# Weight sums of a second projection, formed by transfers in device memory ahead of their use

## The chip, the cores and the metric

The kernel runs on one core of a Trainium2 chip. The metric is the device time of one execution in microseconds (us). A core has the engines TensorE (PE in the profile, with its weight loads as PEld), VectorE (DVE), ScalarE (ACT), GpSimd (POOL) and SyncE (SP), each with its own queue, worked off in order, and 16 transfer engines (DMA) that serve the transfers which SP, ACT and POOL issue. Here SP issues plain transfers and POOL those that add to what stands at their target. SBUF is the memory on the core, PSUM the memory that TensorE writes its products to; inputs and outputs lie in device memory.

## The reference

One layer of a streaming encoder on 1024 tokens of width 1024, in float32:

```python
hn = rmsnorm(h, norm_mix_g[i])
z = hn @ w_in[i]                               # 1024 x 2048
a = pool_mixer(u, pool_w[i], pool_b[i], pool_scale[i])
o = chunk_attention(q, k, v, rel_bias[i])      # 8 heads, own chunk of 64 and 8 before
h = h + jnp.concatenate([a, o], axis=-1) @ w_out[i]
hn = rmsnorm(h, norm_ffn_g[i])
up = hn @ w_up[i]                              # 1024 x 5632: gate, value
gt, val = up[..., :D_FF], up[..., D_FF:]
gt = causal_dwconv(gt, conv_w[i], conv_b[i])
h = h + (jax.nn.gelu(gt, approximate=False) * val) @ w_down[i]   # 2816 x 1024
hn = rmsnorm(h, norm_ple_g[i])
gate = jax.nn.sigmoid(hn @ w_ple_gate[i] + b_ple_gate[i])
h = h + gate * (p[i] @ w_ple[i])
return rmsnorm(h, final_g)
```

The change concerns the product with `w_down`, called the second projection here; the product with `w_up` is the first.

## The kernel before

Everything is kept transposed: channels on the 128 partitions, tokens along the rows. Each float32 factor is split into a rounded part on ACT and a remainder on DVE (`split`, L132 to L134), and a product of two such factors takes three matmuls of 128x128 by 128x512 (`mm3`, L128 to L130).

*Stages.* After the loads and the first norm comes the attention stage (to about 260 us). A loop over 64 pairs of head and token tile puts scores, exponentials and values in order; pieces of the input projection fill TensorE between them. Each head's bias rows are loaded by `load_bias` (SP L319), negated by ACT (L320), and two corners are set by POOL (L321, L322), one head ahead, into one of two buffers; a buffer is free when the head before last is done with it. `load` (SP L180) brings each block of `w_in` and `w_v` into one of two buffers. POOL raises the first norm's sums to the power -0.5 (L246), and clears a few columns ahead of the pooling groups (L443), which are written much later, in `project_u`.

*First projection.* 22 column blocks (`up(fi)`, each with a gate and a value half) are multiplied by the scheme of Strassen and Winograd: the operand of tokens and the weights are cut in quarters, and seven products (`step(fi, n)`, 84 matmuls a block) take the place of eight. POOL adds the quarters of `w_up` in SBUF (L710). Each block's result, GELU of the gate times the value, goes to device memory as one tile of `GD` (SP L869).

*Second projection.* The same scheme on `w_down`, with depth 2816 cut into two halves of 11 tiles. Seven products of 11 steps, 12 matmuls a step, in the order 1, 5, 6, 3, 7, 2, 4, add into PSUM. With w(i,j) the four quarters of the weights, products 5, 6, 3 and 7 need sums:

- product 5: w(2,1) + w(2,2); product 6: that + w(1,1); product 3: that + w(1,2);
- product 7: w(2,1) + w(1,1).

Product 1, 2 and 4 use w(1,1), w(1,2) and w(2,2) themselves. For 5, 6 and 3, `SW(k)` is a resident SBUF tile: loaded in product 5, grown by an adding transfer from POOL (`grown`, L893), and after each use grown again for the next product (`behind`). Product 7 loads a tile and lets one transfer add to it. The other operands are tiles of `GD`: T(k), B12(k) and B22(k) stay in SBUF and are formed into differences by DVE (`later_sums`, L943 to L947), B21 is loaded in product 2. In product 1 the B12 tiles 0 to 6 are loaded all at once, at step 6, and one a step behind that. `ready` issues loads 6 steps ahead, `formed` splits 2 ahead and does the sums of a step 4 steps later (`LAG`). The loads of the gate's weights and their splits (`gate_weights`) are hung into products 7 and 2, and the regions of SBUF that they go to are named anew by `weights_home` and `behind_7`.

*What sets the order.* Only TensorE's order is that of the code (`tc.manual_schedule`). For the other engines a planner runs through the program once and puts on each queue, whenever that queue is free by its reckoning, the instruction that is ready and stands earliest in the code; what is not ready is passed by. A transfer counts there by its size alone, whether it loads, stores, copies or adds. On the chip the order so found is fixed: an instruction that has to wait holds up its queue. `load_to` calls `tc.keep_in_program_order` on its loads once `pinned` is set, behind the first projection, which ties each to the instruction traced before it on SP. Names of the profile: R, B and F are SBUF regions, PS is PSUM, TB and V hold parts of the tokens' operand.

Of the kernel before, what the change touches and what calls it, by code (L numbers as in the profile page):

```python
# [20 lines left out]
NF = FF // P  # L21
# [62 lines left out]
def trunk(tc, xT, pT, vecs, w_qk0, w_in, w_v, bias, counts, pool_w, w_out, w_up, w_down,  # L84
# [4 lines left out]
    with tc.tile_pool(name="sb", bufs=1) as sb, \  # L89
# [14 lines left out]
        small = sb.tile([P, 80], F32, name="small")  # L104
        PS = pp.tile([P, 8, 512], F32, name="PS")
        GD = dr.tile([NF, P, SEQ], F32, name="GD")

        b_pool = tc.tile_pool(name="b1", bufs=1)
        B = b_pool.__enter__().tile([P, 8192], F32R, name="B")
# [653 lines left out]
        for z, d in enumerate((0, 4, 1, 5, 2, 6, 3, 7)):  # L763
            k = z // 2
# [33 lines left out]
        def step(fi, n):  # L798

            x, y, z, w = firsts.get(fi, (0, 1, 2, 3))  # L800
            product({1: x, 2: x, 5: z, 3: z, 6: y, 7: y, 4: w}[n], n not in (2, 3, 7))
            if n == 1 and fi != 1:
                keep(np1, x, -1.0)
            elif n == 2 and fi:
                gate0(x)
                if fi in halved:
                    gate(fi, HS[0])
            elif n == 5:
                keep(rawd if fi == 1 else V[:, HS[1]], z)
# [48 lines left out]
        def up(fi, hook=None):  # L858
            if fi == 0:
                pool.memset(Gb[:, 0:2], 0.0)  # L860
                gate0(firsts[0][0])
            if fi == 1:
                keep(np1, firsts[1][0], -1.0)
            for n in steps[fi]:
                step(fi, n)
                if hook and n == 6:
                    hook()
            values_in(slice(0, SEQ))
            sp.dma_start(GD[fi], Yb)  # L869

# [4 lines left out]
        def raw_buf(which="w"):  # L875
            turn[which] += 1
            return rings[which][turn[which] % len(rings[which])]

        def load_to(dst, src):
            ins = sp.dma_start(dst, src)  # L880
            if pinned[0]:
                tc.keep_in_program_order(ins)
            return dst

        def gated(k, i, j):

            return GD[k + NK * (i - 1), :, HS[2 - j]]

        def weight(k, i, j):
            return w_down[k + NK * (j - 1), :, (i - 1) * 512:i * 512]  # L890

        def grown(dst, k, i, j):
            pool.dma_start(dst, weight(k, i, j), accum_op=ALU.add)  # L893
            return dst

        def T(k):
            return r(2 * k, 512)

        def SW(k):
            return r(96 + 2 * k, 512)  # L900

        def B12(k):
            return r(32 + 2 * k, 512)

        def B22(k):
            return r(64 + 2 * k, 512)

        def operands(n, k):

            if n == 1:  # L910
                if pinned[0]:
                    for z in range(0 if k == READY else k, k + 1):
                        load_to(B12(z), gated(z, 1, 2))
                return load_to(raw_buf(), weight(k, 1, 1)), load_to(T(k), gated(k, 1, 1))
            if n == 5:
                grown(load_to(SW(k), weight(k, 2, 1)), k, 2, 2)
                load_to(B22(k), gated(k, 2, 2))
                return SW(k), T(k)
            if n == 6:
                return SW(k), T(k)  # L920
            if n == 3:
                return SW(k), B22(k)
            if n == 7:
                return grown(load_to(raw_buf(), weight(k, 2, 1)), k, 1, 1), B12(k)
            if n == 2:
                b21[k] = load_to(raw_buf("g"), gated(k, 2, 1))
                return load_to(raw_buf(), weight(k, 1, 2)), b21[k]
            return load_to(raw_buf(), weight(k, 2, 2)), T(k)

        def behind(n, k):  # L930

            if n == 5:
                grown(SW(k), k, 1, 1)
            elif n == 6:
                grown(SW(k), k, 1, 2)
            elif n == 2:
                dve.tensor_tensor(T(k), T(k), b21.pop(k), ALU.subtract)

        def later_sums(n, k):

            tt = dve.tensor_tensor
            if n == 1:
                tt(T(k), T(k), B12(k), ALU.add)  # L943
            elif n == 5:
                tt(T(k), T(k), B22(k), ALU.subtract)
            elif n == 6:
                tt(B12(k), B12(k), B22(k), ALU.subtract)  # L947
# [5 lines left out]
        pinned, b21 = [False], {}  # L953
        ORDER = (1, 5, 6, 3, 7, 2, 4)
        sequence = [(n, k) for n in ORDER for k in range(NK)]
        READY, FORMED, LAG = 6, 2, 4
        got, made = {}, [0, 0]

        def ready(upto):
# [4 lines left out]
        def formed(upto):  # L964
            while made[1] < min(upto, len(sequence)):
                i = made[1]
                w_, g_ = got.pop(i)
                (split_neg if sequence[i][0] in (5, 6) else split)(g_, *g_form[i % 3])
                split(w_, *w_form[i % 4])
                behind(*sequence[i])  # L970
                if i >= LAG:
                    later_sums(*sequence[i - LAG])
                made[1] += 1

        def first_steps():
# [4 lines left out]
        for fi in range(NF):  # L980
            up(fi, first_steps if fi == NF - 1 else None)
        pinned[0] = True
        for z in (1, 2, 3, 4):
            Rs[z] = region(z, F32)
        rings["g"] = [r(b, 512) for b in range(22, 32, 2)]

# [66 lines left out]
        emptied = []  # L1053
# [155 lines left out]
```

## Time and profile before

| | us |
|---|---|
| runs shown (three) | 1169.34, 1169.53, 1166.51; median 1169.34 |
| profiled execution, its own time | 1163.96 |
| its span, first to last instruction | 1162.2 |
| TensorE busy | 1133.5 |
| DVE, ACT, POOL busy | 896.2, 581.6, 249.7 |
| second projection on TensorE | about 801 to 1032 |

The profile is one execution. In a row by stretches stand: the stretch in us from the span's start, its length, the busy time and count of PE, PEld, DVE, ACT and POOL, the granted share of TensorE's clock, the mean busy share of the 16 transfer engines, and GB/s. A row of waits has engine and line, what it waited for, us in total, times, longest. A row in order of time has start, duration, engine, line, operation, target and source, count, and in brackets the idle time before it and what ended it. "SPq" is SP issuing a transfer; "issue" is time in which an engine waited for nothing that the profile shows. A row of transfer issues has count, size and the median time from issue to landing.

### The profile page before, as it was taken

How to read it: one execution, taken by the hardware profiler on the slowest of the kernel's cores; microseconds unless marked ns; L12 is line 12 of the kernel's file. 1: busy time of each engine (PE TensorE's matmuls, PEld its weight loads, DVE VectorE, ACT ScalarE, POOL GpSimd, SP SyncE). 2: the span in 40 equal slices, each digit the busy share in tenths (PEclk: the TensorE clock that was granted, in tenths of full speed). 3: DMA queues.
4: the chain of work that ended last, by engine and by line, in shares of the span. 5: the costliest groups of instructions: out<-in, count | busy, mean ns of one | idle time of the engine just before them, and what ended most of it. 6: DMA issues, size and time to landing. Idle time of an engine off the chain costs nothing.

```text
span 1162.2 us, 15566 instructions
## 1 busy us (share of the span) xinstructions
PE 1133.5 (98%) x5697; PEld 957.3 (82%) x5697; DVE 896.2 (77%) x1396; ACT 581.6 (50%) x1019; POOL 249.7 (21%) x224
## 2 busy tenths in 40 slices
PE   9999999999999999999999999999879999999996
PEld 7988998888888778888888888888757887888996
DVE  7678877879557679999989999988747578974553
ACT  8568687755555434344343433444324465663342
POOL 0000000082013213333434343431135010000000
PEclk9999999999999999999999999999889999999998
DMA  7110101105410361212121222224999265510011
GB/s 261 38 48 30 49 12 67 39 28 181 146 28 10 74 162 61 103 64 100 64 101 64 100 73 91 87 76 140 363 228 151 42 186 179 190 54 1 29 65 53
DMA packets 55660, 111.45 MB, mean 96 GB/s; under 512 B 6304, under 2 KB 8608, under 8 KB 55584
## 3 DMA queue, kind: packets, MB, share of 16 engines
q1 hardware_dynamic: 47376, 95.71, 23.4%
q0 software_dynamic: 8064, 14.68, 7.6%
q8 instruction: 44, 0.72, 0.2%
q14 instruction: 32, 0.26, 0.1%
q10 hardware_dynamic: 144, 0.07, 0.0%
HBM read 94.71 MB, written 15.73 MB: 95 GB/s over the span
## 4 chain that ended last, share of the span: by engine, by line
PE 78%; DMA 7%; DVE 5%; issue 5%; ACT 2%; POOL 1%; SPq 0%; DVEq 0%; POOLq 0%; ACTq 0%
PE PS L129 23%; PE PS L128 23%; PE PS L130 23%; PE PS L366 2%; DVE R L134 2%; DMA R<-in_w_down 2%; PE PS L383 1%; PE PS L384 1%; DMA F<-in_w_up 1%; DMA R<-GD 1%; DMA F<-in_w_down 1%; DMA F<-in_w_gate 1%; POOL R L893 1%; DVE B L134 1%; PE PS L341 1%
## 5 line engine op out<-in xcount | busy, mean ns | idle before, releaser
L128 PE MATMUL PS<-R,R 128*128 128x512 f32 (+1 forms) x944 | 361.9, 383 | 1.6 <-ACT V L796 1.5
L130 PE MATMUL PS<-R,R 128*128 128x512 f32 (+1 forms) x944 | 358.0, 379 | 0.0
L129 PE MATMUL PS<-R,R 128*128 128x512 f32 (+1 forms) x880 | 340.1, 387 | 0.3 <-DVE R L229 0.3
L134 DVE TENSOR_TENSOR R<-F,R 128x512 fp32r<-128x512 f32 (+1 forms) x214 | 189.6, 893 | 26.6 <-ACT R L133 25.9
L130 PEld LDWEIGHTS PS<-R,R 128*128 128x128 f32 x944 | 177.6, 188 | 34.0 <-DVE R L134 0.4
L128 PEld LDWEIGHTS PS<-R,R 128*128 128x128 f32 x944 | 177.7, 188 | 33.8 <-ACT V L796 2.0
L133 ACT ACTIVATE R<-F 128x512 fp32r<-128x512 f32 (+1 forms) x218 | 132.3, 621 | 142.8 <-PE PS L129 81.5
L129 PEld LDWEIGHTS PS<-R,R 128*128 128x128 f32 x880 | 165.7, 188 | 32.2 <-DVE R L229 1.1
L710 POOL TENSOR_TENSOR F<-F 128x512 f32<-128x512 f32 x76 | 142.9, 1880 | 221.9 <-DVE R L134 138.7
L128 PE MATMUL PS<-B 128*128 128x512 f32 x316 | 126.1, 399 | 10.6 <-ACT B L133 5.6
L129 PE MATMUL PS<-B 128*128 128x512 f32 x316 | 126.3, 400 | 2.4 <-DVE B L134 1.2
L130 PE MATMUL PS<-B 128*128 128x512 f32 x316 | 125.3, 397 | 0.0
L134 DVE TENSOR_TENSOR B<-R,B 128x512 fp32r<-128x512 f32 x88 | 59.4, 686 | 36.5 <-ACT B L133 36.2
L133 ACT ACTIVATE B<-R 128x512 fp32r<-128x512 f32 x88 | 53.8, 623 | 61.0 <-PE PS L129 31.6
L128 PEld LDWEIGHTS PS<-B 128*128 128x128 f32 x316 | 60.7, 192 | 25.7 <-ACT B L133 6.9
L129 PEld LDWEIGHTS PS<-B 128*128 128x128 f32 x316 | 60.6, 192 | 19.0 <-DVE B L951 3.3
L129 PE MATMUL PS<-B,R 128*128 128x256 f32 x256 | 72.2, 282 | 0.0
L130 PEld LDWEIGHTS PS<-B 128*128 128x128 f32 x316 | 60.5, 191 | 12.9 <-DVE B L134 0.6
L352 ACT ACTIVATE F<-F,small 128x640 f32<-128x640 f32 (+2 forms) x64 | 44.4, 694 | 21.0 <-DVE small L350 12.8
L128 PE MATMUL PS<-B,R 128*128 128x256 f32 x192 | 54.5, 284 | 0.0
L130 PE MATMUL PS<-B,R 128*128 128x256 f32 x192 | 54.4, 283 | 0.0
L608 ACT ACTIVATE F<-F 128x512 f32<-128x512 f32 (+1 forms) x49 | 27.8, 568 | 47.8 <-DVE F L1112 24.3
(164 smaller groups left out, 1920.1 us busy)
## 6 DMA issues: line engine op xcount, KB each, us to landing
F<-in_w_up SPq DMA_DIRECT2D x91, 256.0 KB, 2.7
GD<-F SPq DMA_DIRECT2D x22, 512.0 KB, 2.6
F<-in_w_down SPq DMA_DIRECT2D x44, 256.0 KB, 4.6
R<-GD SPq DMA_DIRECT2D x44, 256.0 KB, 5.4
R<-in_w_down POOLq DMA_DIRECT2D x33, 256.0 KB, 5.2
F<-in_w_in SPq DMA_DIRECT2D x10, 512.0 KB, 3.5
F<-in_xT SPq DMA_DIRECT2D x16, 256.0 KB, 6.0
F<-in_w_out SPq DMA_DIRECT2D x16, 256.0 KB, 2.8
```

The costliest lines, as they stand in the source:

```text
L128: pe.matmul(ps, ahi, bhi, start=first, stop=False, skip_group_check=more)
L129: pe.matmul(ps, ahi, blo, start=False, stop=False, skip_group_check=more)
L130: pe.matmul(ps, alo, bhi, start=False, stop=last, skip_group_check=more)
L133: act.activation(hi, src, AF.Copy)
L134: dve.tensor_tensor(lo, src, rv(hi), ALU.subtract)
L341: pe.matmul(PS[:, 4 + z, 0:320], q, K1[:, ks], start=False, stop=True)
L352: act.activation(S[:, 0:n], S[:, 0:n], AF.Exp, bias=s_[:, 0:1], scale=-1.0, accum_out=s_[:, 1:2])
L366: pe.transpose(pst[:, j * P:(j + 1) * P], S[:, j * P:(j + 1) * P], ident)
L383: pe.matmul(O, V[:, k, h], pt[:, 0, idx], start=n_ == 0, stop=False)
L384: pe.matmul(O, V[:, k, h], pt[:, 1, idx], start=False, stop=n_ == len(ks) - 1)
L608: act.activation(self.q, src, AF.Square)
L710: pool.tensor_tensor(rawu[to], rawu[a], rawu[b], op)
```

## The change

Four stacks of 11 tiles in device memory, `SD`, hold the sums, and the second projection loads them like plain weights. `weight_sums(k, part)` makes those of one k in six parts, and in the code the parts stand behind the steps of the first projection, part by part in later column blocks (blocks 2 to 17). Its copies are issued by SP, its adding transfers by POOL; none of them is passed to `tc.keep_in_program_order`.

```diff
+        SD = [dr.tile([NF // 2, P, 512], F32, name=f"SD{n}") for n in range(4)]
...
-            for n in steps[fi]:
+            for z, n in enumerate(steps[fi]):
                 step(fi, n)
+                for part in range(6):
+                    k = fi - 2 - part
+                    if z == part and 0 <= k < NK:
+                        weight_sums(k, part)
...
-        def grown(dst, k, i, j):
-            pool.dma_start(dst, weight(k, i, j), accum_op=ALU.add)
-            return dst
+        def weight_sums(k, part):
+
+            s1, s2, s4, s3 = [t[k] for t in SD]
+
+            def grow(t, i, j):
+                pool.dma_start(t, weight(k, i, j), accum_op=ALU.add)
+            if part == 0:
+                sp.dma_start(s1, weight(k, 2, 1))
+                sp.dma_start(s3, weight(k, 2, 1))
+            elif part == 1:
+                grow(s1, 2, 2)
+                grow(s3, 1, 1)
+            elif part == 2:
+                sp.dma_start(s2, s1)
+            elif part == 3:
+                grow(s2, 1, 1)
+            elif part == 4:
+                sp.dma_start(s4, s2)
+            else:
+                grow(s4, 1, 2)
+
+        def weight_sum(n, k):
+            return SD[{5: 0, 6: 1, 3: 2, 7: 3}[n]][k]
...
+            z = {1: k - READY, 5: k + NK - READY}.get(n, -1)
+            if 0 <= z < NK:
+                load_to(B12(z), gated(z, 1, 2))
             if n == 1:
-                if pinned[0]:
-                    for z in range(0 if k == READY else k, k + 1):
-                        load_to(B12(z), gated(z, 1, 2))
                 return load_to(raw_buf(), weight(k, 1, 1)), load_to(T(k), gated(k, 1, 1))
-            if n == 5:
-                grown(load_to(SW(k), weight(k, 2, 1)), k, 2, 2)
-                load_to(B22(k), gated(k, 2, 2))
-                return SW(k), T(k)
...
-                return grown(load_to(raw_buf(), weight(k, 2, 1)), k, 1, 1), B12(k)
+            if n in (5, 6, 3, 7):
+                if n == 5:
+                    load_to(B22(k), gated(k, 2, 2))
+                return load_to(raw_buf(), weight_sum(n, k)), {5: T, 6: T, 3: B22, 7: B12}[n](k)
...
-            if n == 5:
-                grown(SW(k), k, 1, 1)
-            elif n == 6:
-                grown(SW(k), k, 1, 2)
-            elif n == 2:
+            if n == 2:
...
-        READY, FORMED, LAG = 6, 2, 4
+        READY, FORMED, LAG, LAG_1 = 6, 2, 4, 8
...
-                if i >= LAG:
+                if i >= LAG and sequence[i - LAG][0] != 1:
                     later_sums(*sequence[i - LAG])
+                if i >= LAG_1 and sequence[i - LAG_1][0] == 1:
+                    later_sums(*sequence[i - LAG_1])
...
-        for z in (1, 2, 3, 4):
+        for z in (1, 2, 3):
...
         def behind_7():
-            weights_home(2, 32, range(4, 8))
-            Rs[3] = region(3, F32R)
-            hp[0] = [(r(64 + 4 * k, 512), r(66 + 4 * k, 512)) for k in range(KT)]
+            Rs[2] = region(2, F32R)
+            hp[0] = [(r(32 + 4 * k, 512), r(34 + 4 * k, 512)) for k in range(KT)]
...
-        extra = {(3, 10): lambda: weights_home(4, 96, range(4)), (7, 10): behind_7,
-                 (4, 8): norm_a.sums, (4, 9): lambda: norm_a.rows(rst2[:, HS[0]])}
-        for k, at in enumerate([(7, b) for b in (1, 3, 5, 7)] + [(2, b) for b in (1, 3, 5, 7)]):
+        extra = {(6, 10): lambda: weights_home(4, 96, range(4)), (3, 10): lambda: weights_home(3, 64, range(4, 8)),
+                 (7, 10): behind_7, (4, 8): norm_a.sums, (4, 9): lambda: norm_a.rows(rst2[:, HS[0]])}
+        for k, at in enumerate([(3, b) for b in (1, 3, 5, 7)] + [(7, b) for b in (1, 3, 5, 7)]):
```

`SW` goes. B12's tiles are loaded one a step over eleven steps, the sums of product 1's operands are made 8 steps behind instead of 4, and the gate's weights move from products 7 and 2 to products 3 and 7, into regions that are free earlier because `SW` is gone.

More of the change, by code (lines that the diff above doesn't have):

```diff
@@ L890, in weight @@
             return w_down[k + NK * (j - 1), :, (i - 1) * 512:i * 512]
-        def grown(dst, k, i, j):
-            pool.dma_start(dst, weight(k, i, j), accum_op=ALU.add)
-            return dst
+        def weight_sums(k, part):
[18 more added lines that the diff above has]
+            return SD[{5: 0, 6: 1, 3: 2, 7: 3}[n]][k]
         def T(k):
             return r(2 * k, 512)
-        def SW(k):
-            return r(96 + 2 * k, 512)
         def B12(k):
@@ L908, in operands @@
         def operands(n, k):
+            z = {1: k - READY, 5: k + NK - READY}.get(n, -1)
+            if 0 <= z < NK:
+                load_to(B12(z), gated(z, 1, 2))
             if n == 1:
-                if pinned[0]:
-                    for z in range(0 if k == READY else k, k + 1):
-                        load_to(B12(z), gated(z, 1, 2))
                 return load_to(raw_buf(), weight(k, 1, 1)), load_to(T(k), gated(k, 1, 1))
-            if n == 5:
-                grown(load_to(SW(k), weight(k, 2, 1)), k, 2, 2)
-                load_to(B22(k), gated(k, 2, 2))
-                return SW(k), T(k)
[L919 to L923, printed above, removed]
-                return grown(load_to(raw_buf(), weight(k, 2, 1)), k, 1, 1), B12(k)
+            if n in (5, 6, 3, 7):
+                if n == 5:
+                    load_to(B22(k), gated(k, 2, 2))
+                return load_to(raw_buf(), weight_sum(n, k)), {5: T, 6: T, 3: B22, 7: B12}[n](k)
             if n == 2:
```

## The prediction

> **What bounds the kernel now.** I read the page's busy times first, then the stretches around the second projection, then what the engines there wait for, and last the queues of SP, ACT and POOL in the first 80 us, because the transfers that the change adds depend on nothing written late.
>
> ```profile
> PE 1133.5 (98%) x5697; PEld 957.3 (82%) x5697; DVE 896.2 (77%) x1396; ACT 581.6 (50%) x1019; POOL 249.7 (21%) x224
> 720.00:800.00 80.00, 80.00 (x354) 66.27 (x353) 72.34 (x79) 32.81 (x48) 30.32 (x16) 1.00 0.29 102
> 800.00:840.00 40.00, 36.80 (x148) 29.12 (x147) 29.98 (x44) 14.80 (x23) 4.39 (x5) 0.91 0.79 261
> 840.00:880.00 40.00, 32.07 (x119) 23.36 (x119) 24.63 (x41) 12.56 (x22) 16.56 (x19) 0.91 1.00 222
> 880.00:920.00 40.00, 40.00 (x177) 32.83 (x176) 25.66 (x42) 17.03 (x30) 13.05 (x15) 1.00 0.68 109
> 960.00:1000.00 40.00, 38.20 (x166) 30.60 (x165) 36.25 (x60) 26.25 (x48) 0.00 (x0) 1.00 0.60 208
> ```
>
> TensorE is the bound nearly everywhere: 354 matmuls fit into 80 us before the second projection and 177 into 40 us after its worst part, 0.226 us each. Only 800 to 880 falls out: 148 + 119 = 267 matmuls where 354 would fit. The 87 missing ones are 19.7 us. The idle time alone would be 11.1 us; the rest is the granted clock, 0.91. At 960 to 1000, 11 are missing, 2.5 us. So what the second projection can give back is about 22 us.
>
> ```profile
> ACT B L133 <- DMA R<-in_w_down: 27.6, 11, 6.0
> ACT B L133 <- DMA F<-in_w_down: 14.3, 6, 9.6
> 853.82 0.86 POOL L893 DMA_DIRECT2D R<-in_w_down  x1 [3.63 <-issue]
> ```
>
> ACT's splits wait there for weights, above all for those that POOL adds into SBUF (R<-in_w_down), while the transfer engines are fully busy (share 1.00). That is the place the change works on.
>
> **The change part by part.** *The second projection.* The 44 adding transfers leave it. Products 1 and 2 now read 33 + 22 = 55 plain tiles of 256 KB (product 1: weight, T, and B12, whose last six slide into product 2; product 2: s1 and B22). That is 14.4 MB in about 60 us, 240 GB/s, and plain loads have run at 401:
>
> ```profile
> 10.00:15.00 5.00, 4.74 (x24) 3.78 (x25) 4.65 (x8) 4.97 (x9) 0.00 (x0) 1.00 1.04 401
> 860.00:864.00 4.00, 3.61 (x15) 2.64 (x13) 1.93 (x4) 1.78 (x3) 2.60 (x3) 0.91 0.85 142
> 868.00:872.00 4.00, 3.19 (x14) 2.14 (x12) 2.71 (x5) 1.15 (x2) 1.63 (x2) 1.00 0.95 164
> ```
>
> So loads no longer hold ACT there, and the burst of seven B12 loads at one step is spread over eleven steps. Of the 19.7 us I take 18; about 2 us stay, since GD's last tile is stored only after DVE's last product and step 1's first operands come behind it. The additions T + B12 are the same eleven DVE operations, eight steps later and still before product 2 needs them: nothing. The gate weights' 16 loads and splits move one product ahead, into products 3 and 7, where ACT has 17 of 40 us busy and DVE 26 (row 880:920): hidden, and product 2's own loads lose that company, worth 1 of the 2.5 us. Together 19 us gained (between 12 and 22).
>
> *The sums.* Added are 44 plain copies on SP's queue and 44 adding transfers on POOL's, in device memory, in a chain per k: s1 and s3 copied, each added to, s2 copied from s1, added to, s4 copied from s2, added to. In the code they stand in the first projection. But neither SP's nor POOL's order is that of the code. The planner puts next on a queue what is ready first, and here is the trace of it:
>
> ```profile
> 29.72 0.15 POOL L322 MEMSET F<- 64x64 f32 x1
> 30.82 0.12 POOL L443 MEMSET F<- 128x16 f32 x1 [0.95 <-POOL F L322]
> 32.51 0.12 POOL L443 MEMSET F<- 128x16 f32 x1 [1.57 <-DVE F L237]
> 36.62 1.66 POOL L246 TENSOR_TENSOR small<-small 128x8 f32<-128x8 f32 x1 [3.99 <-DVE small L245]
> 197.66 0.12 POOL L443 MEMSET F<- 128x16 f32 x1 [14.03 <-DVE R L273]
> ```
>
> L443 clears the heads of U's groups late in the attention stage; two of the four ran at 30.82 and 32.51, ahead of L246, which stands before the attention loop in the code, because their bytes were free; a third had to wait until 197.66. The copies read an input and write memory that nobody uses, so they are ready from the start. I expect them on SP from about 19 us, right behind the first loads, and the adds and later copies as soon as the planner thinks their sources landed. SP has room there:
>
> ```profile
> 40.02 0.33 SPq L180 DMA_DIRECT2D F<-in_w_in  x1
> 57.50 0.33 SPq L180 DMA_DIRECT2D F<-in_w_in  x1
> 72.85 0.33 SPq L180 DMA_DIRECT2D F<-in_w_v  x1
> 75.13 0.33 SPq L319 DMA_DIRECT2D F<-in_bias  x1
> 77.94 0.74 ACT L320 ACTIVATE F<-F 128x640 f32<-128x640 f32 x1 [0.61 <-DMA F<-in_bias]
> ```
>
> Between 28 and 75 us SP issues four loads. The planner counts an adding transfer like a load, so for it 44 of each fit ahead of the load of head 2's bias at 75.13, which cannot come earlier (its buffer is head 0's). On the chip an adding transfer is slower. SP waits in order: a copy of s2 or s4 holds SP until the add before it has landed, and behind it stand two of the w_in loads, w_v and the bias. The last copy, s4[10], needs the add into s2[10], behind which only about three adds of s4 are left: some 41 adds go first. Their pace:
>
> ```profile
> 845.26 0.89 POOL L893 DMA_DIRECT2D R<-in_w_down  x1 [3.75 <-DMA R<-in_w_down]
> 860.32 0.86 POOL L893 DMA_DIRECT2D R<-in_w_down  x1 [2.11 <-DVE B L951]
> 870.26 0.88 POOL L893 DMA_DIRECT2D R<-in_w_down  x1 [1.51 <-DVE R L947]
> R<-in_w_down POOLq DMA_DIRECT2D x33, 256.0 KB, 5.2
> ```
>
> From 845.26 to 860.32, beside plain loads, there are six steps (the issues between are at 847.30, 849.32, 853.82, 855.32 and 857.34): 2.5 us per add. From 860.32 to 870.26, nearly alone, six steps again: 1.66 us, which the 142 and 164 GB/s above confirm (262,144 bytes in 1.6 to 1.85 us). An add into device memory is not in the trace. Bounds: 0.65 us, if it ran like the plain loads at 401 GB/s, and 3.0 us, if reading the target there costs a fifth more than the slower row. The copies run beside the adds, so the true case lies between the two pace rows; I take their middle, 2.1 us. The adds begin about 30 us, behind the memset of head 1's bias (29.72). Then the bias of head 2 is issued at 30 + 41 x 2.1 + 5.2 (landing) = 121 us instead of 75: 46 us late. ACT has no cover for this: L320 follows at once (77.94) and everything of ACT stands behind it, exponentials and evictions, so TensorE stops a few us later. The lateness of w_in's fourth load (57.50) and of w_v falls into the same stall. By the two pace rows the loss is 28 and 62 us, at 3.0 it is 83, at 0.65 nothing.
>
> The Trainium skill ("DMA: Bandwidth & Descriptors", section "Latency and other measured facts") gives 207 to 214 GB/s for copies within device memory. No run here shows that yet. By it a copy would take an estimated 1.25 us, and if copies did not overlap the adds at all, 44 of them would add 55 us to the loss.
>
> *Sum.* 1163.96 (the profiled execution; span 1162.2) - 19 + 46 = 1191. The median of the runs shown, 1169.34, is 5.4 us above the profiled one; on its scale 1196.
>
> **Rivals.** 1. *The sums are hidden.* Either they stay where they are written, or they run early and nothing waits. In the first projection a column block has 84 matmuls, 19.0 us at 0.226. Four POOL issues of 0.88 us (the L893 rows) fit, since POOL idles 50 of 80 us in row 720:800, and four copies at 0.65 with four adds at 1.66 us raise the transfer share of 0.29 by 9.2 / 19.0 to about 0.8. Then the gain alone is left: 1169 - 19 = 1150. It decides if an add costs under (75 - 5 - 30) / 41 = 1.0 us or the queue keeps the bias ahead of the copies. Against it are the L443 rows and both pace rows. The Trainium skill speaks for it ("DMA: Bandwidth & Descriptors", section "Rules for kernel authors"): issue a transfer early, compute, wait for it late, and its fixed cost is covered. By that rule these sums, needed 700 us later, are free; the L320 row, with no time between its load and it, shows the case where something else stands behind the early transfer.
>
> 2. *The sums stay and slow the first projection.* DVE is busy 72 of 80 us there, and POOL's sums (L710) feed the splits. If each of 16 blocks lost 1 us, the time is 1169 - 19 + 16 = 1166: no change.
>
> 3. *Only part of the chain gets ahead of the bias.* If 28 adds precede it instead of 41, it is issued at 30 + 28 x 2.1 + 5 = 94, 19 us late, which eats the gain: 1169.
>
> 4. *The adds also hold up L246* (36.62) on POOL, which TensorE needs for the norm: some 10 us more, 1206. It is within the range of the forecast.
>
> **How the numbers follow.** The forecast with rival 4 has 0.73, rival 1 has 0.17, rivals 2 and 3 together 0.10, of which 0.06 end within 0.3% (3.5 us, about what this measurement can tell), 0.02 above and 0.02 below. So faster 0.19, same 0.06, slower 0.75. The forecast's own range goes from a loss of 28 and a gain of 22, 1175, to a loss of 83 and a gain of 12, 1240. To leave out no more than 2 in 10 the range must reach rival 1: 1150 to 1240.
>
> **What would show it.** Right: copies on SP from about 20 us; adds on POOL before L246 or soon behind; a load of head 2's bias past 100 us; ACT's L320 with tens of us of idle time put down to that load, and slices of idle TensorE near 80 to 120 us; at the second projection about 177 matmuls in every 40 us and no adds. Wrong: adds on POOL between 440 and 750 us, or the third bias load still near 75 us. A bias load at 121 with the stall away from it would refute the place, not the sum.

## The result, and the profile after

The changed kernel takes 1209.45 us, the median of four runs (1208.15 to 1213.74), against 1167.92 for the kernel before beside it: a ratio of 1.0362, 95% interval 1.0328 to 1.0395. It is slower by 41.5 us. The profiled execution took 1210.64 us, its span is 1208.9; the one of the kernel before took 1163.96 (span 1162.2), some 4 us under its median, so the two profiles lie 46.7 us apart. Lines of the changed kernel stand one higher than before up to the first projection: the bias load is L320, its negation L321, the norm's power L247, a split L134 and L135, POOL's sums L711. The new copies are L904, L905 (first level), L910 and L914 (second and third), the adds L902, the store to GD L874.

First the page's busy times and the stretches of the front (all that comes ahead of the first store to GD); columns as in the prediction's rows.

```profile
PE 1128.2 (93%) x5697; PEld 958.1 (79%) x5697; DVE 893.9 (74%) x1396; ACT 582.0 (48%) x1019; POOL 247.9 (21%) x224
```

```profile
80.00:100.00 20.00, 9.01 (x52) 7.46 (x50) 4.75 (x12) 4.16 (x9) 5.78 (x8) 0.80 0.98 217
100.00:120.00 20.00, 0.00 (x0) 0.00 (x0) 0.00 (x0) 0.00 (x0) 7.40 (x9) 0.50 0.99 197
120.00:140.00 20.00, 0.00 (x0) 0.00 (x0) 0.00 (x0) 0.00 (x0) 5.76 (x7) 0.50 0.95 191
140.00:160.00 20.00, 13.87 (x73) 12.39 (x74) 11.58 (x30) 10.82 (x25) 1.11 (x3) 0.75 0.24 47
```

From 89 to 146 us TensorE does nothing, ACT and DVE stand from about 86 to 144, and the transfer engines are full up to 140 us (0.95 to 0.99). The waits of the first 300 us say for what, in three answers for ACT, PE and SP:

```profile
ACT F L321 <- DMA F<-in_bias: 59.0, 3, 58.5
```

```profile
PE PS L367 <- DVE B L375: 58.0, 3, 57.1
PE PS L292 <- POOL small L247: 4.3, 1, 4.3
```

```profile
SPq L914 <- DMA SD<-in_w_down: 52.5, 11, 7.4
SPq L910 <- DMA SD<-in_w_down: 27.9, 11, 5.9
```

ACT waits 58.5 us for head 2's bias. That load was late because SP stood at its copies: 22 of them waited together 52.5 + 27.9 = 80.4 us for adds to land. In order of time (start, duration, engine, line; one answer each for SP, ACT and POOL):

```profile
25.32 0.60 SPq L904 DMA_DIRECT2D SD<-in_w_down  x1
...
126.84 9.72 SPq L914 DMA_DIRECT2D SD<-SD  x3
...
137.29 0.37 SPq L320 DMA_DIRECT2D F<-in_bias  x1
```

```profile
143.37 0.74 ACT L321 ACTIVATE F<-F 128x640 f32<-128x640 f32 x1 [58.46 <-DMA F<-in_bias]
```

```profile
29.16 1.04 POOL L902 DMA_DIRECT2D SD<-in_w_down  x1 [1.00 <-DMA SD<-in_w_down]
...
43.07 1.97 POOL L247 TENSOR_TENSOR small<-small 128x8 f32<-128x8 f32 x1
...
141.16 0.81 POOL L902 DMA_DIRECT2D SD<-in_w_down  x1 [3.02 <-DMA SD<-SD]
```

All 88 transfers of the sums run from 25 to 144 us, ahead of and inside the attention stage. The bias load, at 75.13 before, comes at 137.29. The norm's power, at 36.62 before, comes at 43.07 behind six adds.

The second projection, where the change was to help:

```profile
840.00:880.00 40.00, 38.68 (x171) 31.68 (x170) 35.19 (x43) 17.28 (x26) 7.34 (x4) 1.00 0.37 121
880.00:920.00 40.00, 39.68 (x175) 32.53 (x174) 35.34 (x59) 17.68 (x30) 0.00 (x0) 1.00 0.87 307
...
1000.00:1040.00 40.00, 40.00 (x178) 33.10 (x178) 37.01 (x61) 26.01 (x47) 0.00 (x0) 1.00 0.56 187
```

Its rows hold 171 to 178 matmuls where before two had 148 and 119. The work that stood in the row 960:1000 before (166 matmuls) is done some 47 us later here, in the row 1000:1040 (178). Three landmarks, the same in every kernel, give the balance: the first store to GD, the last one, and the last addition to H behind the second projection (L1026, before L1012). Starts in us, and the two differences:

| kernel | first GD store | last GD store | first projection | last H addition | second projection | span |
|---|---|---|---|---|---|---|
| before | 408.56 | 808.92 | 400.4 | 1035.63 | 226.7 | 1162.2 |
| after | 475.94 | 877.83 | 401.9 | 1082.44 | 204.6 | 1208.9 |

The front lost 67.4, the first projection 1.5, the second projection gained 22.1: together 46.8, within 0.1 of the difference of the spans.

### The profile page after: what moved, and what is told of

Read it like the earlier page. It is cut to its first block, busy times and chain, and to the rows that moved or that the text cites. A ratio compares the mean times of both kernels' runs of the same rounds, so it can differ in the third digit from the quotient of the medians.

```text
span 1208.9 us, 15677 instructions
## 1 busy us (share of the span) xinstructions
PE 1128.2 (93%) x5697; PEld 958.1 (79%) x5697; DVE 893.9 (74%) x1396; ACT 582.0 (48%) x1019; POOL 247.9 (21%) x224
## 4 chain that ended last, share of the span: by engine, by line
PE 53%; issue 3%; DMA 2%; DVE 2%; ACT 1%; SPq 0%; DVEq 0%; POOLq 0%; POOL 0%; ACTq 0%
PE PS L130 17%; PE PS L129 17%; PE PS L131 17%; DMA F<-in_w_up 1%; DMA F<-in_w_down 1%; DVE R L135 1%; DVE F L835 0%; PE PS L617 0%; ACT R L134 0%; ACT F L834 0%; DVE F L841 0%; DVE V L820 0%; PE PS L625 0%; SPq L885 0%; DVE B L135 0%
## 5 line engine op out<-in xcount | busy, mean ns | idle before, releaser
L135 DVE TENSOR_TENSOR R<-F,R 128x512 fp32r<-128x512 f32 (+1 forms) x214 | 190.9, 899 | 32.0 <-ACT R L134 31.4
L134 ACT ACTIVATE R<-F 128x512 fp32r<-128x512 f32 (+1 forms) x218 | 132.0, 620 | 151.2 <-PE PS L130 73.8
L711 POOL TENSOR_TENSOR F<-F 128x512 f32<-128x512 f32 x76 | 142.9, 1880 | 222.6 <-DVE R L135 152.0
L130 PE MATMUL PS<-B 128*128 128x512 f32 x316 | 123.3, 390 | 1.6 <-DVE B L135 1.6
L129 PE MATMUL PS<-B 128*128 128x512 f32 x316 | 123.2, 390 | 0.0
L131 PE MATMUL PS<-B 128*128 128x512 f32 x316 | 123.1, 389 | 0.0
L134 ACT ACTIVATE B<-F 128x512 fp32r<-128x512 f32 (+1 forms) x86 | 55.7, 648 | 77.5 <-PE PS L130 54.2
L367 PE MATMUL PS<-ident,F 128*128 128x128 f32 x240 | 37.7, 277 | 58.2 <-DVE B L375 58.0
L367 PEld LDWEIGHTS PS<-ident,F 128*128 128x128 f32 x240 | 29.1, 142 | 67.1 <-DVE B L375 61.7
L135 DVE TENSOR_TENSOR B<-F,B 128x512 fp32r<-128x512 f32 (+1 forms) x86 | 61.0, 710 | 26.4 <-ACT B L134 26.1
L621 POOL TENSOR_TENSOR small<-small 128x4 f32<-128x4 f32 (+1 forms) x7 | 7.7, 1096 | 338.3 <-DVE small L620 338.3
L130 PE MATMUL PS<-B,R 128*128 128x256 f32 x256 | 73.2, 286 | 0.0
L130 PEld LDWEIGHTS PS<-B 128*128 128x128 f32 x316 | 59.3, 188 | 14.7 <-DVE B L135 2.5
L129 PEld LDWEIGHTS PS<-B 128*128 128x128 f32 x316 | 59.3, 188 | 12.4
L131 PEld LDWEIGHTS PS<-B 128*128 128x128 f32 x316 | 59.3, 188 | 12.3
L354 DVE RECIPROCAL small<-small 128x1 f32<-128x1 f32 x64 | 10.3, 161 | 74.3 <-ACT F L353 73.8
```

Of the source, the lines that this page charges most:

```text
L129: pe.matmul(ps, ahi, bhi, start=first, stop=False, skip_group_check=more)
L130: pe.matmul(ps, ahi, blo, start=False, stop=False, skip_group_check=more)
L131: pe.matmul(ps, alo, bhi, start=False, stop=last, skip_group_check=more)
L134: act.activation(hi, src, AF.Copy)
L135: dve.tensor_tensor(lo, src, rv(hi), ALU.subtract)
L354: dve.reciprocal(s_[:, 2:3], s_[:, 1:2])
```

## The experiments

Two theories stood at first for the loss in the front. *Order*: the loads of the attention stage stand on SP behind copies that wait for adds. *Company*: 88 transfers fill the transfer engines, and loads land late whatever the queue. For what the sums would cost in their written place, the question was open. The landmarks of all runs (us):

| kernel | time | ratio to before, 95% interval | first GD store | first projection | second projection |
|---|---|---|---|---|---|
| e1 tied to their places | 1186.34 | 1.0148 (1.0128 to 1.0168) | 409.4 | 441.6 | 204.9 |
| e2 other queue | 1187.58 | 1.0154 (1.0129 to 1.0180) | 449.5 | 400.9 | 204.6 |
| e3 no sums | 1143.90 | 0.9783 (0.9764 to 0.9802) | 409.5 | 402.1 | 205.0 |
| e4 sums alone | 1234.33 | single run | 476.2 | 401.0 | 229.1 |
| e5 plain transfers | 1178.64 | single run | 444.7 | 401.8 | 204.0 |
| e6 spread loads alone | 1167.68 | 0.9991 (0.9976 to 1.0007) | 409.1 | 400.8 | 227.3 |
| e7 tied, copies a block later | 1168.15 | 0.9999 (0.9983 to 1.0016) | 410.6 | 425.5 | 204.9 |
| e8 first level | 1156.29 | 0.9892 (0.9864 to 0.9920) | 418.1 | 402.0 | 204.7 |
| e9 tied, two blocks a part | 1171.84 | 1.0026 (1.0010 to 1.0043) | 410.5 | 427.1 | 204.3 |
| e10 two levels | 1172.15 | 1.0033 (1.0014 to 1.0051) | 412.5 | 427.6 | 207.8 |
| e11 copies behind the loads | 1148.47 | 0.9837 (0.9816 to 0.9858) | 409.5 | 406.4 | 204.2 |
| e12 adds moved too | 1148.29 | 0.9836 (0.9820 to 0.9853) | 409.1 | 405.8 | 204.4 |

### The two parts apart: e3, e4, e6

e3 takes the sums out of the changed kernel; products 5, 6, 3 and 7 load a quarter of the weights in their place:

```diff
-                        weight_sums(k, part)
+                        pass
...
-            return SD[{5: 0, 6: 1, 3: 2, 7: 3}[n]][k]
+            return weight(k, *{5: (2, 2), 6: (1, 1), 3: (1, 2), 7: (1, 1)}[n])
```

> The changed kernel without the sums: nothing is copied or added, and products 5, 6, 3 and 7 load a quarter of the weights where the sum would be (so the second projection computes something else with the same transfers and matmuls). It gives the second projection's part alone. If the parts add up: 1168 - 22 = 1146, with the attention stage as before (first store of GD near 409 us). If the early sums had also helped or hurt the second projection by other ways: off 1146 by more than 5.

It takes 1143.90: the second projection as it became is 21.7 us shorter (226.7 to 205.0), and nothing else changes by more than 2 us.

e4 puts the sums, unused, into the kernel before:

```diff
-            for n in steps[fi]:
+            for z, n in enumerate(steps[fi]):
                 step(fi, n)
+                for part in range(6):
+                    k = fi - 2 - part
+                    if z == part and 0 <= k < NK:
+                        weight_sums(k, part)
```

> The kernel before, with its own second projection, and beside it the 88 transfers of the sums as the change has them; nobody reads their results. The front's part alone: 1168 + 67 = 1235, first store of GD near 476 us instead of 409, ACT's wait for head 2's bias 58 us. If the changed second projection had a share in the early order (through the region names or the later loads), the front would be late by clearly less.

1234.33, with the first store to GD at 476.2, as in the changed kernel. So the sums cost 67 us in the front and 3 behind it (0.6 in the first projection, 2.4 in the second), and the two parts add up: 1143.9 + 67 = 1211.

e6 is the kernel before with B12's loads one a step and product 1's sums 8 steps behind; adds into SBUF stay.

```diff
+            z = {1: k - READY, 5: k + NK - READY}.get(n, -1)
+            if 0 <= z < NK:
+                load_to(B12(z), gated(z, 1, 2))
...
-        READY, FORMED, LAG = 6, 2, 4
+        READY, FORMED, LAG, LAG_1 = 6, 2, 4, 8
```

> The kernel before with two parts of the change alone: the B12 tiles are loaded one a step over eleven steps, and the sums of product 1's operands are made 8 steps behind. No SD; the adds into SBUF stay. If the burst of B12 loads made product 1's share of the second projection's loss by itself (about 7 of the 22 us, at 800 to 840) and the adds the rest, the time is 1169 - 7 = 1162. If both come from the adds into SBUF, nothing changes: 1169. If the burst is the cause of both, 1148.

No change. In its stretches

```profile
800.00:840.00 40.00, 37.44 (x156) 29.79 (x155) 29.66 (x44) 15.44 (x24) 5.26 (x6) 0.96 0.78 252
840.00:880.00 40.00, 30.70 (x110) 21.92 (x109) 23.78 (x40) 11.41 (x20) 15.53 (x18) 0.91 1.03 235
```

stand 156 + 110 = 266 matmuls where the kernel before has 148 + 119 = 267: the loads moved, and the same loss came later. So spreading the loads by itself gains nothing while the adds into SBUF stay; the gain of 22 us needs the adds out of the second projection. What the spreading, or the gate's weights moved to other products, adds once they are out was not run.

### What makes the front late: e2, e5, e8

e2 takes the loads of bias and input weights off SP's queue, and the corners off POOL's:

```diff
-            sp.dma_start(t, src)
+            act.dma_start(t, src)
...
-            sp.dma_start(b, bias[h])
+            act.dma_start(b, bias[h])
...
-            pool.memset(b[0:64, 576:640], BIG)
-            pool.memset(b[64:128, 0:64], BIG)
+            dve.memset(b[0:64, 576:640], BIG)
+            dve.memset(b[64:128, 0:64], BIG)
```

> The changed kernel with the sums early as they are, but the loads of bias, w_in and w_v issued by ACT, and the two corners of each bias set by DVE. The transfers' traffic from 25 to 140 us stays the same. If the bias only stood in SP's line: ACT's wait of 58 us goes to a few us, the 7 us at the norm's power stay (that is POOL's line), and the time is 1168 + 7 - 22 = 1153, up to 1160 with somewhat slower loads. If the saturated transfer engines are what makes loads late, whatever queue issues them: loads take tens of us, and the time stays above 1185.

1187.58: the front is 41 us late instead of 67. The time is what the company theory foresaw, but the trace shows other reasons than its own. ACT's waits of the first 300 us, then a stretch:

```profile
ACT F L356 <- DMA SD<-SD: 23.1, 1, 23.1
...
ACT F L321 <- DMA F<-in_bias: 7.0, 2, 4.5
```

```profile
100.00:120.00 20.00, 20.00 (x108) 17.12 (x107) 15.02 (x37) 12.49 (x26) 6.56 (x8) 0.94 1.04 233
```

The wait for the bias is gone (58.5 to 4.5), and TensorE runs full beside full transfer engines (20.00 of 20 at 1.04). So company alone does not stop it. Two other waits took the place: the norm's power came later still on POOL (53 instead of 43 us, more adds ahead of it), and ACT stood 23 us at a load of `w_in` that it now issues itself, with L356, the row's line, right behind it; the trace names a copy (SD<-SD) as its releaser. Why that load depends on a copy was not settled. A load moved to ACT's queue can hold up ACT, as these 23 us do.

e8 keeps the transfers on SP and POOL, and makes the first level alone, so that no copy waits for an add (products 6 and 3 then load s1 in place of s2 and s4):

```diff
-                for part in range(6):
+                for part in range(2):
...
-            return SD[{5: 0, 6: 1, 3: 2, 7: 3}[n]][k]
+            return SD[{5: 0, 6: 0, 3: 0, 7: 3}[n]][k]
```

> The changed kernel with only the first level of sums, s1 and s3: 22 copies and 22 adds, so no copy on SP waits for an add (the second and third sums are left out: products 6 and 3 load s1). The transfers still float ahead of the attention stage. If SP's copies waiting for adds are what holds the bias load, it is issued near 75 to 80 us, ACT does not wait for it, only L246 behind some adds on POOL may be late by up to 7 us: time 1147 to 1155. If the mere number of early transfers holds the stage up, half of the chain is left and with it about half of the 67 us: 1180.

1156.29, just above the 1147 to 1155 of the order theory: half of the transfers leave not half of the 67 us but 9. On SP, and in PE's waits:

```profile
80.89 0.33 SPq L320 DMA_DIRECT2D F<-in_bias  x1
```

```profile
PE PS L292 <- POOL small L247: 3.9, 1, 3.9
```

The bias load is 6 us late instead of 62, and no copy holds it: as in the kernel before, SP waits there for the buffer of head 0, and head 0 is 6 us late because POOL's power comes at 42.17, nearly as late as in the changed kernel. The load then takes 6.8 us to land (L321 starts at 87.64) where it took 2.8 before, beside transfer engines that are full (0.97 from 60 to 80), and ACT waits 4.5 us for it. So of the 9.5 us that the front loses, about 6 are the power's and most of the rest the slower landing's; company costs that much. The chain is also half as long here and its last add is issued at 79.72, so e8 alone doesn't part order from number. With the changed kernel's rows, where 80.4 us of SP go by at copies ahead of the bias, and with e2 it says that order counts: a queue holding copies that wait for adds.

e5 keeps count, order and dependences of all 88 transfers and makes the adds plain:

```diff
-                pool.dma_start(t, weight(k, i, j), accum_op=ALU.add)
+                pool.dma_start(t, weight(k, i, j))
```

> The changed kernel with every adding transfer turned into a plain transfer of the same 256 KB from POOL's queue (the sums are left out: each tile of SD ends as the last quarter written). The number of transfers, their order on every queue and their dependences stay. Theory (the pace of adds into device memory sets how late head 2's bias is issued): a plain packet of 2 KB takes 84 ns in the trace of the changed kernel, one that adds 178, so the chain runs about twice as fast, 43 x 1.2 instead of 112 us from 29 on, and the bias is issued at 80 to 95 instead of 137; ACT waits for it 0 to 20 us, and the time is 1150 to 1172. Rival (what holds SP is the count of transfers and of the waits between them, each with a landing of some 3 to 5 us): the bias stays past 120, ACT's wait above 40 us, the time above 1190.

1178.64, a single run, between the two: the bias is issued at 104.88, ACT waits 33.1. POOL's 44 transfers start from 28.27 to 108.09, 79.8 / 43 = 1.86 us apart, against (141.16 - 29.16) / 43 = 2.60 with adds. Why neither number was foreseen is read from the transfers by queue (packets, MB, share of the 16 engines; q0 carries POOL's, q1 SP's). The changed kernel from 25 to 144 us, then e5 from 25 to 110:

```profile
q0 software_dynamic: 6241, 11.38, 60.2%
q1 hardware_dynamic: 4736, 14.29, 37.5%
```

```profile
q1 hardware_dynamic: 4736, 14.29, 52.2%
q0 software_dynamic: 3466, 11.38, 41.2%
```

The bytes are the same, and both shares sum to over 93%: the engines are full, and the pace is about what they can do. An add of 256 KB takes 0.602 x 119 us x 0.262 / 11.38 = 1.65 us of all sixteen; plain, 0.412 x 85 x 0.262 / 11.38 = 0.81 us; a copy of SP's as much (0.375 x 119 x 0.262 / 14.29 = 0.82). For each add there is one copy: 1.65 + 0.82 = 2.47, and the other loads make 2.60; plain 0.81 + 0.82 = 1.63, with them 1.86. POOL's plain transfers go in larger packets than its adds (3466 against 6241), but that is not what makes them faster: in the changed kernel's trace a plain packet of 2 KB on SP's queue takes 84 ns (median), one of 2 KB that adds 178. So the chain is about as slow as the transfer engines, and it costs what stands behind it in order.

### What the sums cost in their written place: e1, e7, e9 to e12

e1 ties all 88 to the order of the code, so that nothing floats ahead:

```diff
-                pool.dma_start(t, weight(k, i, j), accum_op=ALU.add)
+                tc.keep_in_program_order(pool.dma_start(t, weight(k, i, j), accum_op=ALU.add))
```

(and so the copies).

> The changed kernel with every copy and every add of the sums tied to the instruction traced before it on its queue, so that they stay in the first projection. If the loss comes from the order of the queues alone: head 2's bias is issued near 75 us again, ACT's wait for it falls from 58 us to about 1, TensorE's wait for the norm's power (4 us) goes, and the 22 us of the second projection remain: some 1146 us, ratio to before 0.98. If the sums' transfers cost time wherever they run (splits and POOL sums of the first projection held up, 1 us in each of 16 column blocks): about 1162.

1186.34, far above both numbers expected. The front is as before (409.4), but the first projection is 41 us longer. SP's waits from 440 to 880 us, then one block on SP and on POOL:

```profile
SPq L910 <- DMA SD<-in_w_down: 49.3, 11, 5.1
```

```profile
611.25 0.48 SPq L910 DMA_DIRECT2D SD<-SD  x1
611.82 0.53 SPq L874 DMA_DIRECT2D GD<-F  x1
612.40 0.50 SPq L904 DMA_DIRECT2D SD<-in_w_down  x1
612.96 1.06 SPq L905 DMA_DIRECT2D SD<-in_w_down  x1
614.11 1.81 SPq L702 DMA_DIRECT2D F<-in_w_up  x3
```

```profile
606.25 1.68 POOL L902 DMA_DIRECT2D SD<-in_w_down  x2
...
622.20 1.28 POOL L711 TENSOR_TENSOR F<-F 128x512 f32<-128x512 f32 x1 [9.72 <-DMA F<-in_w_up]
```

The adds are issued at 606.25, and SP waits for them with L910 until 611.25, ahead of the store to GD and three loads of `w_up`. In the code a block lies between an add and the copy that reads it. But the weights of the first projection are fetched and summed three products ahead: on POOL the adds stand behind sums of later products, and on SP the copy stands ahead of the store of the block before. So the block between them is gone: when SP comes to the copy the adds have only just been issued, and it stands until one has landed (611.25 - 606.25 = 5.0 us).

e7 keeps e1's ties and puts the copies that read a sum one more block behind its add.

```diff
-                    k = fi - 2 - part
+                    k = fi - 2 - 2 * (part // 2)
```

> The kernel with the sums tied to their places (e1), with one more column block between an add and the copy that reads its target. If the first projection of e1 lost its 41 us because SP stood at a copy until the add issued a few us before had landed, with the loads of w_up behind it, that wait ends: first projection about 400 us from the first to the last store to GD, time 1146 to 1150, the fastest of all. If the adds themselves slow the first projection (bandwidth, or POOL's time for issuing them), it stays near 440 us, time above 1175.

1168.15: 16 of the 41 us come back, 25 stay. SP no longer waits for adds; POOL now waited for copies, since copy and add into the same tile are left in one block (37 us in all). e9, tied too, widens every gap:

```diff
-                    k = fi - 2 - part
+                    k = fi - 1 - 2 * part
```

> The kernel with the sums tied to their places, now with one more column block behind each of the six parts, also between a copy and the add into its target (e7 left that pair in one block, and POOL stood there 37 us in all until copies had landed). If waits of SP and POOL for transfers issued shortly before are all that the tied order costs, the first projection takes 400 to 405 us from its first to its last store, and the time is 1146 to 1152. If POOL's time for issuing the adds (0.83 us each, 4 a block, between sums that the splits wait for) or the transfers' company is what is left of e7's 25 us, the first projection takes 415 to 425 us and the time is 1158 to 1168.

1171.84, the first projection 427.1, above both expectations: nothing gained, although SP and POOL no longer wait there with copies and adds. The wait that e7 showed was cover for another. And e10, as e9 but with eleven copies and eleven adds fewer there, is no better:

```diff
-                for part in range(6):
+                for part in range(4):
...
+                if n == 3:
+                    pool.dma_start(t, weight(k, 1, 2), accum_op=ALU.add)
```

> As e9, without the last level: s4 is not made; product 3 loads s2, and one adding transfer a step puts w(1,2) onto it in SBUF, as product 7 had it before. 11 copies and 11 adds fewer in the first projection, 11 adds more in the second. If each add in the first projection costs POOL time that the splits wait for, a quarter of e9's remaining loss there is saved, and product 3, where loads are few, hides its adds: 2 to 5 us below e9. If e9 has no loss left, equal to it (within 2 us), or slower where product 3 has to wait for its adds.

1172.15, first projection 427.6, second 3 us longer. So neither the waits nor the number of adds made the rest. The trace of e9, SP and POOL in one block, and its transfers from 480 to 700 us (KB each, median us to landing):

```profile
577.11 0.33 SPq L874 DMA_DIRECT2D GD<-F  x1
577.49 0.50 SPq L904 DMA_DIRECT2D SD<-in_w_down  x1
578.04 0.85 SPq L905 DMA_DIRECT2D SD<-in_w_down  x1
578.99 2.91 SPq L702 DMA_DIRECT2D F<-in_w_up  x3
```

```profile
588.53 1.28 POOL L711 TENSOR_TENSOR F<-F 128x512 f32<-128x512 f32 x1 [9.54 <-DMA SD<-SD]
```

```profile
F<-in_w_up SPq DMA_DIRECT2D x41, 256.0 KB, 5.8
```

The loads stand behind two copies, issued just ahead of them, and behind a 512 KB store. They take 5.8 us to land. The kernel before has 2.6, and in one block SP and POOL run

```profile
F<-in_w_up SPq DMA_DIRECT2D x48, 256.0 KB, 2.6
```

```profile
561.72 0.33 SPq L869 DMA_DIRECT2D GD<-F  x1
563.41 14.17 SPq L701 DMA_DIRECT2D F<-in_w_up  x4
```

```profile
567.54 1.29 POOL L710 TENSOR_TENSOR F<-F 128x512 f32<-128x512 f32 x1 [4.71 <-DMA F<-in_w_up]
```

POOL's first sum of the block, on which the next splits and products hang, starts 588.53 - 577.11 = 11.4 us behind the store in e9; in the kernel before, 567.54 - 561.72 = 5.8. (The row puts its wait down to a copy issued right behind the loads, which the sum doesn't read; fourteen other such waits, 96.9 us together, are put down to the loads.) e11 keeps e9's gaps and ties and moves the copies behind the loads:

```diff
-                    if z == part and 0 <= k < NK:
+                    if z == (part if part % 2 else 4) and 0 <= k < NK:
```

> As e9, with one thing moved: SP issues the copies behind the three loads of w_up of a block instead of ahead of them (the adds stay). In e9 a load of w_up takes 5.8 us to land instead of 2.6, two copies issued directly ahead of it, and POOL's first sum of a block waits for it; ten blocks lose about 2.5 us each. If those copies ahead of the loads are the cause, a load lands in about 3 us again, the first projection takes 400 to 408 us, and the time is 1146 to 1154. If it is the adds in flight or POOL's time for issuing them, nothing changes: 420 to 427 us and 1164 to 1172.

```profile
565.57 0.33 SPq L874 DMA_DIRECT2D GD<-F  x1
567.27 2.73 SPq L702 DMA_DIRECT2D F<-in_w_up  x3
570.06 0.50 SPq L904 DMA_DIRECT2D SD<-in_w_down  x1
```

```profile
572.98 1.29 POOL L711 TENSOR_TENSOR F<-F 128x512 f32<-128x512 f32 x1 [5.52 <-DMA F<-in_w_up]
```

1148.47, ratio 0.9837: a load lands in 4.1 us (median, not the 3 expected), the sum starts 7.4 us behind the store (9.1 in the next block), and the first projection is 6 us longer than before instead of 27. From 480 to 680 us, before, e9 and e11 in this order:

```profile
480.00:680.00 200.00, 200.00 (x884) 165.66 (x883) 183.95 (x191) 80.32 (x116) 78.39 (x42) 1.00 0.24 85
```

```profile
480.00:680.00 200.00, 189.91 (x802) 147.46 (x801) 159.56 (x170) 73.29 (x106) 94.33 (x67) 1.00 0.58 147
```

```profile
480.00:680.00 200.00, 199.34 (x874) 162.97 (x873) 178.16 (x187) 79.99 (x114) 102.40 (x73) 1.00 0.61 159
```

The transfers' share is about the same in e9 and e11 (0.58 and 0.61); their place in the order makes the difference. It is not SP's time for issuing the two copies (1.4 us a block), since SP has to wait behind the store anyway: the first load goes out 1.70 us behind the store in e11 (567.27 - 565.57), 1.69 before, and 1.88 in e9. What e9 loses is the landing of the loads. The Trainium skill ("DMA: Bandwidth & Descriptors", section "Queues, rings and completion order") says that SP's transfers share one ring on each of the 16 transfer engines, which is consumed in order. The trace agrees: 5.8 us to landing behind the copies, 4.1 ahead of them.

e12 moves the adds into a stretch where the engines were idle:

```diff
-                    if z == (part if part % 2 else 4) and 0 <= k < NK:
+                    if z == (5 if part % 2 else 4) and 0 <= k < NK:
```

> As e11, and the adds moved too: POOL issues them behind its first sum of a block, when the trace of e9 shows the transfer engines idle, instead of behind the third and fourth, just ahead of the store and the loads. If adds in flight slow the loads of w_up, this gains what e11 leaves, 2 to 15 us, and ends at 1146 to 1150. If the copies were all, it equals e11 within 2 us. If POOL's time for issuing holds up the next sums (3.3 us a block where four are issued, against a gap of 4.4 us before), it is up to 10 us slower than e11.

Its loads of `w_up` land in 2.8 us, but the time is that of e11 (1148.29): what loads still lost in e11 was covered. Both beat the kernel before by 1.6%; e3, which makes no sums at all, stands at 0.9783, about 6 us lower.

## Why the prediction was right, and where its terms were off

The forecast was 1196 us within 1150 to 1240, most likely slower; 1209.45 came.

- *The sums float to the front.* Right, and by the L443 rows it was read from. The first copy came at 25.32, not 19: it stood behind the bias load at 24.94, not right behind the first loads.
- *SP is held in order, and the bias of head 2 pays.* Right in place and mechanism: 80.4 us of SP's time at copies waiting for adds, ACT 58.5 us at L321. e8 shows that without such copies the same queue issues the bias at 80.89; e2, that full transfer engines alone do not stop TensorE.
- *The pace of 2.1 us an add* is the term that was mis-sized. It was the middle of a row alone (1.66) and one beside loads (2.5), on the argument that copies run beside adds. They do, but on engines that are full: each add brings a copy of its own, and their times add up, 1.65 + 0.82. Measured 2.60 from first to last; the 41 intervals ahead of the bias, from 29.16 on, took 103.9 us instead of 86. So the bias came at 137.29 and not at 121. The rows for this sum were at hand: 1.66 for an add and 0.65 for a plain load make 2.31, ahead of all other loads.
- *The loss of 46 us* was 67.4. Of the 21 us that were missing, 16 are the bias issued later. Some 3 are its landing, 143.37 - 137.29 = 6.1 us beside full transfer engines instead of 77.94 - 75.13 = 2.8, which the sum had at its old length. The last 2 come behind L321, up to the first store to GD.
- *Rival 4*, priced at 10 and left out of the sum, came as well: the power at 43.07 instead of 36.62, the first scores at 63.25 instead of 55.63, 7.6 us. But it is no term to add to the bias, as its price of 1206 had it. ACT comes to L321 that much later and waits that much less: L321 is 143.37 - 77.94 = 65.4 us late, and 58.5 of waiting with the 7.6 make 66.1, where 0.6 was waited before. In e8, where no copy holds the bias, the same delay is seen, and makes about 6 of the 9.5 us.
- *The gain of 19 us* was 22.1; e3 gives 21.7. About 2 us stay at the seam of the two projections (171 and 175 matmuls), as said; the work of the row 960:1000 gained all of its 2.5 us, not 1. By e6, spreading the burst of B12 gains nothing alone.
- *Sum.* 1163.96 + 67.4 + 1.5 - 22.1 = 1210.8, the profiled execution's 1210.64. The errors of 21 in the loss and 3 in the gain worked against each other, so profile to profile the forecast was 20 us low (1191 against 1210.64). By the medians it comes nearer, 1196 against 1209.45, and that is luck: the 5.4 us added for the scale are not there in the changed kernel, whose profiled execution lies 1.2 us above its median.
- *The copies' rate.* e5 moved 25.7 MB in 85 us, 303 GB/s, 23.1 of them by the 88 plain transfers within device memory, and a copy took 0.8 us of the engines. The estimate of 1.25 us a copy, by the Trainium skill's 207 to 214 GB/s ("DMA: Bandwidth & Descriptors", section "Latency and other measured facts"), does not hold for these tiles. The Trainium skill has these rates for two row pitches, 512 KiB and 4 MiB with 4 KiB of padding. What the prediction named with it, copies and adds that do not overlap, is what happened, because the engines were full.
- *Rival 1* (hidden, 1150) did not come true for this kernel, but its price did: e11 gives 1148.47. The Trainium skill's rule of issuing early and waiting late ("DMA: Bandwidth & Descriptors", section "Rules for kernel authors") says that a transfer's fixed cost is covered. In e11, with nothing urgent right behind the sums, all but some 6 us of the sums' time was covered; in the changed kernel SP's next loads stood behind them, and 67 us were lost.
- *Rival 2* (sums stay, the first projection pays 16 us) has a true core: it paid 41 in e1, 25 to 27 in e7 and e9, 6 in e11. But the engine named, DVE, was not the way; it was SP waiting for adds in e1, and the loads of `w_up` behind the copies in e9.

## What to carry to other kernels

A transfer that needs nothing late is not free because its result is needed late: a planner that fills queues with what is ready puts it ahead of urgent loads, and a chain of them makes a queue that works in order wait. Before moving such work, list what stands behind each of its instructions on its queue, keep every wait far from its cause as the queues run and not as the code reads, and put the transfers behind the loads on which the next product hangs. When two streams share full transfer engines, add their times; don't take one as cover for the other. When two delays meet at one wait, as the power and the bias here, don't add them: the later one counts.

## What the runs showed of the hardware beyond expectation

- An adding transfer takes twice the time of the transfer engines that a plain one takes: 1.65 against 0.81 us per 256 KB within device memory. Into SBUF it is about the same: in the kernel before, nearly alone from 860 to 872 us,

```profile
q0 software_dynamic: 1004, 1.83, 90.5%
```

  which is 0.905 x 12 x 0.262 / 1.83 = 1.56 us. So the target's place made little difference here.
- While TensorE waited, its granted clock read 0.50 (100 to 140 us), and 0.75 in the 20 us in which it went on (row 140:160).
- The same 88 transfers, the same bytes, cost 67 us in the front of the changed kernel and 41 (e1), 25 (e7) or 6 (e11) in the first projection, by their place in the queues alone.
